# Shift and scale of an expert layer's tokens: from full-width rows to per-feature columns

## The chip, the core and the metric

The kernel runs on one core of a Trainium2 chip. The metric is device microseconds of one execution. The chip works through five engines that run side by side, each through its own queue: TensorE (PE, with its weight loads as PEld), VectorE (DVE), ScalarE (ACT), GpSimd (POOL) and SyncE (SP). Sixteen DMA engines move data between HBM and the on-chip memory SBUF; transfers are issued from the queues of SP, ACT and POOL. TensorE writes to PSUM, which DVE and ACT read.

## The reference

The model is three transformer-like blocks over 256 tokens of 1024 features. Each block has a mixer and, behind it, a mixture of experts; the change lies in how the tokens reach the experts:

```python
h2 = _rms(x) * norm2_w * (1.0 + sc2) + sh2          # shift and scale per feature
x = x + g2 * hier_moe(h2, ...)                      # 32 experts, 2 per token, d_ff 512
...
h = modulate(rms_norm(x, norm_ffn_g[i]), sh2, sc2)  # h * (1 + scale) + shift
x = x + g2[:, None, :] * hier_moe_2(h, ...)         # 16 experts, 2 per token, d_ff 256
```

So a token's input to its experts is `x * r * s + sh`, where `r` is one number per token (the reciprocal root mean square), and `s` and `sh` are one number per feature.

## The kernel before

`body` (line 2314) runs `block1`, an expert phase (`moe_phase`, line 1870, called m1 here after its tile names), the mixer `mla`, a second expert phase (n0), the mixer `hyena`, and a third (n1). The 256 tokens stand as two tiles of 128 partitions, `x[:, t]`, with 1024 features each.

An expert phase works as follows. The weights of its experts stream through a ring of six slots of 2 MB, which SP loads in order as slots come free (`moe_stream`, line 1819): 201 MB in m1, 50 MB in n0 and n1 each. At the start, GpSimd fills a tile `zero`, writes it to the buffer `Y` in HBM (four transfers of 512 KB), and loads two rows of 1024 values from HBM, `shrow` and `srow`, each spread over all 128 partitions (512 KB a row, `row_in`, line 857, called at line 1922). These rows were written to HBM earlier by `moe_prep` (line 864) through `rows_out` (line 845), which transposes 16 columns of 128 on TensorE, copies them on ScalarE and stores them from GpSimd's queue. The same values stand in SBUF as columns: tile `mcols`, one value per feature, eight columns each for the shift and the scale.

`ffn_in` (line 1754) computes `r` (`rms_rows`, a chain of small VectorE instructions, lines 742 to 764), transposes the tokens, scales them by the columns while they leave PSUM, and makes the router's logits on TensorE (line 1773). `ffn_rows` (line 1777) makes the experts' input for all tokens: GpSimd multiplies by `srow` (line 1783), VectorE by `r` and adds `shrow` (line 1784), ScalarE rounds to the matmul's type (`h2h`, line 1786). `Route.choose` (line 137) picks two experts per token, on VectorE and with five small matmuls; `onehot` (line 222) makes the gathering matrix. Behind it the remainder `h2l = h - h2h` is taken, for one token tile on VectorE and for the other on GpSimd (line 1931, by the constant `LOP`).

`Moe.start` (line 495) then gathers the tokens of the first eight experts. For each of eight k-tiles of 128 features, four matmuls (`gather`, line 251: `h2h` and `h2l`, two token tiles) fill a PSUM bank of 128 features by 512 slots, and ScalarE copies it to a tile `xg` (`gathered`, line 263). Only then does the first expert's product with its weights begin (`up_unit`, line 287). Later groups of eight experts are gathered between the experts' matmuls (line 545): three groups in m1, one in n0 and n1 each. The order of each engine's instructions is fixed at build time: the framework places them, `tc.issue_after` puts a block behind a named instruction of the same engine, and the expert loop keeps the written order.

Of the kernel before, what the change touches and what calls it, by code (L numbers as in the profile page):

```python
# [15 lines left out]
F32 = mybir.dt.float32  # L16
# [4 lines left out]
AF = mybir.ActivationFunctionType  # L21
ALU = mybir.AluOpType
# [4 lines left out]
D = 1024  # L27
T = 256
P = 128
# [192 lines left out]
def onehot(k, pool, r, g, tag):  # L222

    oh = k.t(pool, [P, 2, GE, CAP], F32R, tag)
    for t in range(2):
        k.chosen = k.nc.vector.tensor_tensor(
            oh[:, t], r.posm[:, t, g * GE:(g + 1) * GE, None].to_broadcast([P, GE, CAP]),
            k.io64[:, None, :].to_broadcast([P, GE, CAP]), op=ALU.is_equal)
    return oh


class Moe:
# [30 lines left out]
    def gathered(self, g, c, n=None):  # L263

        k, nc = self.k, self.nc
        n = n or GE
        xg = self.xg[g][c] = k.t(self.sb, [P, n * CAP], F32, "xg", bufs=XG)
        self.gathers = nc.scalar.activation(xg, self.gp, AF.Copy)  # L268

    def state(self, e):  # L270
        return self.st.setdefault(e, {})
# [573 lines left out]
def rows_out(k, pool, cols, name):  # L845

    nc, n = k.nc, cols.shape[1]
    d = k.tc.dram_tile([n, P], F32, name=name)
    pt = k.fbank()
    nc.tensor.transpose(pt[:n, :P], cols, k.ident)  # L850
    s = k.t(pool, [n, P], F32, "rowst")
    nc.scalar.copy(s, pt[:n, :P])
    nc.gpsimd.dma_start(d, s)
    return d.rearrange("(n c) p -> n (c p)", c=8)


def row_in(k, pool, d, i, name):

    o = k.t(pool, [P, D], F32, name)
    k.nc.gpsimd.dma_start(o, d[i:i + 1].broadcast_to([P, D]))  # L860
    return o


def moe_prep(k, pool, l, g, ada, wr, br):

    nc, NL = k.nc, wr.shape[2]
    cols = k.t(k.const, [P, 16], F32, f"mcols{l}")
    nc.vector.tensor_copy(cols[:, 0:8], ada[:, 24:32])
    nc.vector.scalar_tensor_tensor(cols[:, 8:16], ada[:, 32:40], 1.0, g, op0=ALU.add, op1=ALU.mult)
    pt = k.fbank()  # L870
    for c in range(8):
        nc.tensor.matmul(pt[:, :NL], ada[:, 24 + c:25 + c].to_broadcast([P, P]), wr[:, c], start=(c == 0), stop=(c == 7))
    crow = k.t(k.const, [P, NL], F32, f"crow{l}")
    nc.vector.tensor_tensor(crow, pt[:, :NL], br, op=ALU.add)
    return dict(s=cols[:, 8:16], crow=crow, rows=rows_out(k, pool, cols, f"mrows{l}"), wr=wr)


def cond_pads(k, cs):
# [449 lines left out]

FTK = 2
EVD = '0123'  # L1330
PSTT = 0
AHEAD = 0

TWO_PI = (6.28125, 0.0019350051879882812, float(2 * np.pi - 6.28125 - 0.0019350051879882812))
# [439 lines left out]
    return pl, r  # L1774


def ffn_rows(k, tmp, x, r, srow, shrow, h2h):

    nc = k.nc
    hs = []  # L1780
    for t in range(2):
        h = k.t(tmp, [P, D], F32, "h2", bufs=2)
        k.rowed = nc.gpsimd.tensor_tensor(h, x[:, t], srow, op=ALU.mult)
        i = (nc.gpsimd if PSTT else nc.vector).scalar_tensor_tensor(h, h, r[:, t:t + 1], shrow, op0=ALU.mult, op1=ALU.add)
        k.rowed = i if PSTT else k.rowed
        nc.scalar.activation(h2h[:, t], h, AF.Copy)  # L1786
        hs.append(h)
    return hs


PLAN = "rrrraaaarafaaarffaaaaafa|ooaooao"
# [9 lines left out]
NRB = 2  # L1801
ORD = "3f2f4ffhckrff1f0f"
FB = [1, 2, 2, 2]
LOP = [1]
MAN = ['None', '0', '1']
RINGS = {'n0': 6, 'n1': 6}

# [62 lines left out]
def moe_phase(k, I, x, l, M, after=None, store=None):  # L1870

    nc, tc = k.nc, k.tc
    NE, FF = (32, 512) if l is None else (16, 256)
    pre = "m1" if l is None else f"n{l}"
    with ExitStack() as es:
        ph = Phase(k, es)
        k.psum(es, acc=4, bank=4)
        k.fill = "acc"
        hp = ph(pre + "h")
        if l is None:  # L1880
            ring = [ph(f"ring{i}") for i in range(4)] + [ph(f"ring{i}", side="right") for i in range(4, 6)]
            S = Stream(k, es, "ring", 6, 4096, homes=[ring[int(c)] for c in RO])
        else:
            S = Stream(k, es, "ring", RINGS[pre], 4096)
        moe_stream(k, I, S, l)
        S.upto(S.depth + len(S.once))
        views = {}

        def load(kind, e, u):

            key = (kind, e, u // 4 if kind == "d" else u // 2) if l is None else (kind, e)
            if key not in views:
                views[key] = S.get(key)
            v = views[key]
            if kind != "d":
                return (lambda a, c: v[:, a, c % 4]) if l is None else (lambda a, c: v[:, c, a * 256:(a + 1) * 256])
            return v[:, :, u % 4] if l is None else v[:, u // 2, :, u % 2]

        def fetch(w, kind, e, u):
            if l is None and kind == "d":  # L1900
                h, c = divmod(u, 2)
                src = I["w2"][ds(e, 1), h][:, :, 2 * c:2 * c + 2]
            elif l is None:
                src = I["w13"][ds(e, 1), u // 2][:, :, "gu".index(kind), u % 2 * 2:u % 2 * 2 + 2]
            elif kind == "d":
                src = I["moe_w_down_2"][l, ds(e, 1), u]
            else:
                src = I["moe_w_in"][l, ds(e, 1)][:, :, 2 * u:2 * u + 2]
            nc.sync.dma_start(w, src.rearrange("a p c f -> p (a c) f"))

        h2h, h2l = k.t(hp, [P, 2, D], F32R, "h2h"), k.t(hp, [P, 2, D], F32R, "h2l")
        with ExitStack() as e1:
            if l is None:
                k.t(ph("pad", es=e1), [P, PAD * 256], F32, "pad")
            rp = ph(pre + "r", es=e1, side="left" if l is None else "right")
            tmp = ph(pre + "t", es=e1)
            Y = tc.dram_tile([2 * T, D], F32, name=pre + "Y")
            zero = k.t(rp, [P, D], F32, "zero")
            nc.gpsimd.memset(zero, 0.0)
            for c in range(2 * T // P):  # L1920
                nc.gpsimd.dma_start(Y[c * P:(c + 1) * P], zero)
            shrow, srow = (row_in(k, rp, M["rows"], i, n) for i, n in enumerate(("shrow", "srow")))
            pl, r = ffn_in(k, tmp, rp if l is None else tmp, x, M)
            R = Route(k, hp, NE, NE // 4, pre)
            hs = ffn_rows(k, tmp, x, r, srow, shrow, h2h)
            R.choose(pl, r, M["crow"])
            oh = onehot(k, hp, R, 0, "oh0")
            with tc.issue_after(k.chosen.ins):
                last = k.rowed
                for t in range(2):  # L1930
                    i = (nc.gpsimd if t in LOP else nc.vector).tensor_tensor(h2l[:, t], hs[t], h2h[:, t].bitcast(F32), op=ALU.subtract)  # L1931
                    if t in LOP:
                        last = i
                    else:
                        low = i
        with ExitStack() as e1:
            m = Moe(k, e1, pre, R, h2h, h2l, load, NE, FF, Y)
            m.fetch = fetch
            m.low = low
            m.start(oh)  # L1940
            with tc.issue_after(m.gathers.ins):
                R.gates()
            run = m.run()
            with (tc.manual_schedule() if str(l) in MAN else ExitStack()):
                next(run)
            if after:
                with tc.issue_after(m.ready.ins), tc.issue_after(last.ins), ExitStack() as e2:
                    after(ph("pl", 2, es=e2))
            with (tc.manual_schedule() if str(l) in MAN else ExitStack()):
                list(run)  # L1950
            op = m.vpool = ph(pre + "o", es=e1)
            with tc.issue_after(last.ins):
                g2 = row_in(k, op, M["g2"], 0, "g2row")
            for h, t in ((0, 0), (0, 1), (1, 0), (1, 1)):
                y, c = k.t(op, [P, 2, 512], F32, "vw", bufs=2), slice(h * 512, (h + 1) * 512)
                with tc.issue_after(m.sent.ins):
                    nc.gpsimd.dma_start(y, Y.rearrange("(c t p) d -> t p c d", c=2, p=P)[t][:, :, c])
                with tc.issue_after(m.acted.ins):
                    nc.vector.tensor_tensor(y[:, 0], y[:, 0], y[:, 1], op=ALU.add)
                    nc.vector.tensor_tensor(y[:, 0], y[:, 0], g2[:, c], op=ALU.mult)  # L1960
                    nc.vector.tensor_tensor(x[:, t, c], x[:, t, c], y[:, 0], op=ALU.add)

            def add():
                for h in range(2):
                    residual(k, op, x, [m.acc[t][h] for t in range(2)], g2, h)
                    if store:
                        store(h)

            add()
            m.overflow(add)  # L1970
            k.newt = None
# [404 lines left out]
```

## Time and profile before

| What | Value |
|---|---|
| median of three runs | 1531.34 us (1524.98 to 1534.3) |
| the profiled execution | 1536.42 us, of which the span in the profile is 1534.7 us |
| busy share of the span: PE, DVE, ACT, POOL | 86%, 36%, 30%, 8% |
| TensorE's mean granted clock | 0.922 of full speed |
| moved by DMA | 462.18 MB, 301 GB/s over the span |
| experts begin (first line 287): m1, n0, n1 | 346.74, 1078.37, 1409.62 us |

Times inside the profile count from the start of the span. The share of busy time is a mean over stages with different limits, so each expert phase is read by itself. In the rows below, a name such as `h<-xres,srow` gives the tile written and the tiles read, and a bracket at the end of a timeline row says how long the engine had been idle and what ended that.

### The profile page before, as it was taken

To read this page: it belongs to the slowest core of one execution; us is meant where nothing else is said; L and a number is where in the kernel's file an instruction comes from. 1 tells how busy PE (TensorE), PEld (TensorE's weight loads), DVE (VectorE), ACT (ScalarE), POOL (GpSimd) and SP (SyncE) were. 2 spreads that over 40 slices of the span, in tenths; PEclk is the share of its full clock that TensorE was granted. 3 is DMA by queue.
4 is the path that set the end of the run, shared out by engine and by line. 5 is a ranking of instruction groups with operands and counts; after the bars stand their busy time and mean duration, and the time that the engine had idled before them with its cause. 6 is when DMAs were issued, how large, how long until landed. Compare 5 with 4: busy or idle time off the path is not lost. (4 is left out here: it accounts for less than half of the span.)

```text
span 1534.7 us, 18651 instructions
## 1 busy us (share of the span) xinstructions
PE 1319.7 (86%) x7228; PEld 761.0 (50%) x7228; DVE 546.5 (36%) x1522; ACT 461.6 (30%) x906; POOL 116.2 (8%) x153
## 2 busy tenths in 40 slices
PE   5898999939989999989988397991999399987995
PEld 2676686623345453323322164661554388766552
DVE  2563665440321320000000556442102577765004
ACT  2463343311223322112111253430232255423221
POOL 0000000020111210000000100011001000102000
PEclk9799899959999999999999688995999599997998
DMA  8457714458998999999999567476799665729996
GB/s 330 174 201 258 265 66 165 172 217 351 414 400 337 345 336 421 424 425 424 425 424 423 216 236 258 165 262 272 309 418 417 230 245 204 263 104 384 410 420 235
DMA packets 65904, 462.18 MB, mean 301 GB/s; under 512 B 9782, under 2 KB 10134, under 8 KB 33680
## 3 DMA queue, kind: packets, MB, share of 16 engines
q1 hardware_dynamic: 52496, 424.97, 70.2%
q0 software_dynamic: 12880, 35.21, 6.1%
q8 instruction: 60, 0.98, 0.3%
q10 hardware_dynamic: 432, 0.72, 0.2%
q14 instruction: 36, 0.29, 0.1%
HBM read 444.04 MB, written 25.74 MB: 306 GB/s over the span
## 5 line engine op out<-in xcount | busy, mean ns | idle before, releaser
L287 PE MATMUL bank<-ring,xg 128*64 128x512 f32 (+1 forms) x2048 | 354.3, 491 | 19.1 <-DMA ring<-in_w_dram 16.6
L287 PEld LDWEIGHTS bank<-ring,xg 128*64 128x64 f32 x2048 | 142.2, 137 | 205.7 <-issue 135.4
L377 PE MATMUL bank<-ring,a 128*64 128x512 f32 x768 | 204.9, 602 | 7.6 <-DMA ring<-in_w_dram 7.5
L310 DVE TENSOR_TENSOR a<-bank,sg 128x256 f32<-128x256 f32 (+1 forms) x64 | 22.9, 358 | 475.0 <-ACT sg L305 290.3
L818 DVE TENSOR_TENSOR wl<-ra,wh 128x1024 fp32r<-128x1024 f32 (+1 forms) x77 | 93.3, 1216 | 77.7 <-ACT wh L816 76.7
L816 ACT ACTIVATE wh<-ra 128x1024 fp32r<-128x1024 f32 (+1 forms) x77 | 80.7, 1053 | 112.6 <-PE acc L831 38.5
L377 PEld LDWEIGHTS bank<-ring,a 128*64 128x64 f32 x768 | 55.1, 136 | 103.2 <-issue 88.0
L292 ACT ACTIVATE s<-bank 128x512 f32<-128x512 f32 (+1 forms) x64 | 31.4, 491 | 248.7 <-PE bank L287 248.7
L898 PE MATMUL fill<-rb,cpad 128*32 128x512 f32 x384 | 67.8, 655 | 27.4 <-DMA rb<-in_ada_w_dram 19.6
L259 PE MATMUL bank<-oh,h2h 128*128 128x512 f32 x128 | 48.1, 459 | 48.4 <-ACT h2h L1786 47.3
L366 ACT ACTIVATE y<-bank,gts 128x512 f32<-128x512 f32 x54 | 37.1, 688 | 75.9 <-PE bank L377 75.9
L268 ACT ACTIVATE xg<-bank 128x512 f32<-128x512 f32 x64 | 38.3, 598 | 68.8 <-PE bank L259 68.8
L259 PEld LDWEIGHTS bank<-oh,h2h 128*128 128x128 f32 x128 | 25.0, 213 | 66.9 <-ACT h2h L1786 48.9
L1688 PE MATMUL acc<-hTh,wh 128*128 128x256 f32 x192 | 55.7, 293 | 0.0
L1688 PE MATMUL acc<-hTh,wl 128*128 128x256 f32 x192 | 55.4, 294 | 0.2 <-DVE wl L818 0.2
L1688 PE MATMUL acc<-hTl,wh 128*128 128x256 f32 x192 | 54.1, 285 | 0.0
L305 ACT ACTIVATE sg<-bank 128x256 f32<-128x256 f32 (+1 forms) x64 | 21.0, 328 | 91.6 <-PE bank L299 91.6
L259 PE MATMUL bank<-oh,h2l 128*128 128x512 f32 x128 | 44.3, 432 | 1.6 <-POOL h2l L1931 1.6
L299 PEld LDWEIGHTS bank<-ident,s 128*128 128x128 f32 x192 | 19.8, 140 | 46.3 <-issue 36.2
L831 PE MATMUL acc<-wh,hTh 128*128 128x512 f32 (+1 forms) x96 | 39.6, 412 | 3.6 <-ACT hTv L800 3.6
L1662 PE MATMUL acc<-ftk,dftf 128*128 128x128 f32 x256 | 36.0, 287 | 7.6 <-ACT ftk L1656 7.6
L1662 PEld LDWEIGHTS acc<-ftk,dftf 128*128 128x128 f32 x256 | 30.8, 192 | 22.1 <-ACT ftk L1656 12.0
(689 smaller groups left out, 2132.3 us busy)
## 6 DMA issues: line engine op xcount, KB each, us to landing
ring<-in_w_dram SPq DMA_DIRECT2D x64, 2048.0 KB, 18.9
ring<-in_moe_w_in_dram SPq DMA_DIRECT2D x32, 2048.0 KB, 17.6
ring<-in_w_dram SPq DMA_DIRECT2D x62, 1024.0 KB, 17.8
rb<-in_ada_w_dram SPq DMA_DIRECT2D x48, 1024.0 KB, 5.2
ring<-in_moe_w_down_dram SPq DMA_DIRECT2D x32, 1024.0 KB, 18.6
rb<-in_w_mod_dram SPq DMA_DIRECT2D x16, 1024.0 KB, 7.6
ra<-in_hy_w_in_dram SPq DMA_DIRECT2D x12, 1024.0 KB, 8.8
ra<-in_w_in_dram SPq DMA_DIRECT2D x20, 512.0 KB, 3.8
```

The source lines that it names most:

```text
L259: i = nc.tensor.matmul(self.gp, h[:, t, c * P:(c + 1) * P], oh[:, t], start=(a == t == 0), stop=(a == t == 1))
L268: self.gathers = nc.scalar.activation(xg, self.gp, AF.Copy)
L287: self.nc.tensor.matmul(s["p"][a * CAP:(a + 1) * CAP, :self.FF], x, w(a, c), start=(c == 0), stop=(c == 7))
L292: self.nc.scalar.activation(s["s"], s["p"][:, :self.FF], AF.Copy)
L366: nc.scalar.activation(s["y"][:, h * 512:(h + 1) * 512], s["d", h], AF.Copy, scale=s["gt"])
L377: self.nc.tensor.matmul(q["d", h][i * CAP:(i + 1) * CAP], self.state(2 * p + i)["av"][:, c], w[:, i], start=(c == 0), stop=(c == nk - 1))
L816: k.last[0] = k.nc.scalar.activation(wh[:, :, :n], w, AF.Copy)
L818: k.last[1] = k.nc.vector.tensor_tensor(wl[:, :, :n], w, wh[:, :, :n].bitcast(F32), op=ALU.subtract)
L831: k.last[2] = k.nc.tensor.matmul(out, x, y[:, j, c0:c0 + n], start=(kt == 0 and a == 0), stop=(kt == KT - 1 and a == 2))
L898: nc.tensor.matmul(pr[32 * g:32 * g + 32], k.cpad[:, l, 4 * q + g], wq[:, g], start=(q == 0), stop=(q == 1))
L1662: nc.tensor.matmul(pt[:, (2 * f + n) * P:(2 * f + n + 1) * P], self.fwd[:, t, n, f * P:(f + 1) * P], tk[:, n, t], start=(t == 0), stop=(t ...
L1688: nc.tensor.matmul(acc[i][:, :T], y[:, jj, i * P:(i + 1) * P], self.hT[x][:, kt], start=(kt == 0 and a == 0), stop=(kt == 7 and a == 2))
```

## The change

The rows are dropped. The tokens are only normalised before the gather (`x * r`, on ScalarE, straight into `h2h`), and their remainder is taken on VectorE by one instruction per half tile, `x * r - h2h`, behind the gathering matrix. The scale and the shift are applied as the gathered k-tile leaves PSUM: there the features lie on partitions, so ScalarE takes both as one value per partition. A gathered slot that no token fills now holds the shift instead of zero; its output goes nowhere, as before. `rows_out` of the 16 columns, both `row_in` loads, GpSimd's products and its half of the remainder go away.

```diff
     def gathered(self, g, c, n=None):
-        self.gathers = nc.scalar.activation(xg, self.gp, AF.Copy)
+        self.gathers = nc.scalar.activation(xg, self.gp, AF.Identity, scale=self.scale[:, c:c + 1], bias=self.shift[:, c:c + 1])
...
     # moe_prep
-    return dict(s=cols[:, 8:16], crow=crow, rows=rows_out(k, pool, cols, f"mrows{l}"), wr=wr)
+    return dict(s=cols[:, 8:16], sh=cols[:, 0:8], crow=crow, wr=wr)
...
-def ffn_rows(k, tmp, x, r, srow, shrow, h2h):
+def ffn_rows(k, x, r, h2h, h2l):
     nc = k.nc
-    hs = []
     for t in range(2):
-        h = k.t(tmp, [P, D], F32, "h2", bufs=2)
-        k.rowed = nc.gpsimd.tensor_tensor(h, x[:, t], srow, op=ALU.mult)
-        i = (nc.gpsimd if PSTT else nc.vector).scalar_tensor_tensor(h, h, r[:, t:t + 1], shrow, op0=ALU.mult, op1=ALU.add)
-        k.rowed = i if PSTT else k.rowed
-        nc.scalar.activation(h2h[:, t], h, AF.Copy)
-        hs.append(h)
-    return hs
+        nc.scalar.activation(h2h[:, t], x[:, t], AF.Copy, scale=r[:, t:t + 1])
+
+    def second():
+        for h in range(2):
+            for t in range(2):
+                c = slice(h * 512, (h + 1) * 512)
+                i = nc.vector.scalar_tensor_tensor(h2l[:, t, c], x[:, t, c], r[:, t:t + 1], h2h[:, t, c].bitcast(F32),
+                                                   op0=ALU.mult, op1=ALU.subtract)
+        return i
+    return second
...
     # moe_phase
-            shrow, srow = (row_in(k, rp, M["rows"], i, n) for i, n in enumerate(("shrow", "srow")))
             pl, r = ffn_in(k, tmp, rp if l is None else tmp, x, M)
             R = Route(k, hp, NE, NE // 4, pre)
-            hs = ffn_rows(k, tmp, x, r, srow, shrow, h2h)
+            second = ffn_rows(k, x, r, h2h, h2l)
             R.choose(pl, r, M["crow"])
             oh = onehot(k, hp, R, 0, "oh0")
             with tc.issue_after(k.chosen.ins):
-                last = k.rowed
-                for t in range(2):
-                    i = (nc.gpsimd if t in LOP else nc.vector).tensor_tensor(h2l[:, t], hs[t], h2h[:, t].bitcast(F32), op=ALU.subtract)
-                    if t in LOP:
-                        last = i
-                    else:
-                        low = i
+                last = second()
...
             m.fetch = fetch
-            m.low = low
+            m.scale, m.shift = M["s"], M["sh"]
```

## Rows read from the trace of the kernel before

**Rows 1.** Waits in n0: engine, tile, line <- releaser: us, times, longest.
```profile
POOL h L1783 <- DMA srow<-mrows: 26.3, 1, 26.3
```

**Rows 2.** Timeline of m1's start: start us, us, engine, line, operation [idle before <-releaser].
```profile
315.03 1.29 DVE L226 TENSOR_TENSOR oh<-m1posm,io 128x512 fp32r<-128x512 f32 x2
...
327.30 4.64 POOL L1783 TENSOR_TENSOR h<-xres,srow 128x1024 f32<-128x1024 f32 x2 [19.80 <-DMA srow<-mrows]
...
333.05 2.25 ACT L1786 ACTIVATE h2h<-h 128x1024 fp32r<-128x1024 f32 x2 [24.26 <-DVE h L1784]
...
334.16 1.99 PE L259 MATMUL bank<-oh,h2h 128*128 128x512 f32 x3 [19.43 <-ACT h2h L1786]
...
346.74 10.52 PE L287 MATMUL bank<-ring,xg 128*64 128x512 f32 x48
```

**Rows 3.** Windows in m1: length, busy us PE PEld DVE ACT POOL, clock, DMA, GB/s.
```profile
323.00:326.00 3.00, 0.00 (x0) 0.00 (x0) 0.00 (x0) 0.00 (x0) 0.00 (x0) 0.50 0.92 377
...
328.00:336.00 8.00, 1.84 (x4) 1.05 (x5) 6.29 (x4) 2.11 (x2) 4.56 (x3) 0.50 0.00 0
```

**Rows 4.** Timeline of n0's start, same columns as rows 2.
```profile
1032.07 0.16 DVE L749 TENSOR_SCALAR rxi<-rxv 128x2 int32<-128x2 int32 x1
...
1039.16 1.29 DVE L226 TENSOR_TENSOR oh<-n0posm,io 128x512 fp32r<-128x512 f32 x2
...
1066.77 1.99 PE L259 MATMUL bank<-oh,h2h 128*128 128x512 f32 x3 [27.87 <-ACT h2h L1786]
...
1078.37 5.40 PE L287 MATMUL bank<-ring,xg 128*64 128x256 f32 x48
...
1082.08 1.54 SPq L1841 DMA_DIRECT2D ring<-in_moe_w_down_dram  x2
```

**Rows 5.** Windows of n0's wait and gather, same columns as rows 3.
```profile
1058.00:1060.00 2.00, 0.00 (x0) 0.00 (x0) 0.00 (x0) 0.00 (x0) 0.10 (x1) 0.50 0.96 410
...
1061.00:1070.00 9.00, 2.84 (x5) 1.33 (x5) 5.70 (x3) 2.12 (x2) 5.55 (x3) 0.50 0.01 5
...
1073.00:1074.00 1.00, 1.00 (x4) 0.76 (x4) 0.00 (x0) 0.18 (x1) 0.00 (x0) 0.67 0.21 86
```

**Rows 6.** Timeline of n1's start and one row of its end, same columns as rows 2.
```profile
1382.90 5.05 POOL L1783 TENSOR_TENSOR h<-xres,srow 128x1024 f32<-128x1024 f32 x2 [0.45 <-DVE xres L842]
...
1384.28 1.38 DVE L742 SCALAR_TENSOR_TENSOR rxv<-rxq 128x2 f32<-128x2 f32 x1
...
1385.97 2.01 DVE L749 TENSOR_SCALAR rxi<-rxv 128x2 int32<-128x2 int32 x1
...
1390.29 2.48 DVE L1784 SCALAR_TENSOR_TENSOR h<-h,rxy,shrow 128x1024 f32<-128x1024 f32 x2
...
1394.32 2.01 DVE L124 TENSOR_TENSOR n1ae<-n1ae,n1af 128x40 f32<-128x40 f32 x1
...
1398.83 1.29 DVE L226 TENSOR_TENSOR oh<-n1posm,io 128x512 fp32r<-128x512 f32 x2
...
1399.67 2.04 PE L259 MATMUL bank<-oh,h2h 128*128 128x512 f32 x4 [1.10 <-DVE oh L226]
...
1409.62 5.40 PE L287 MATMUL bank<-ring,xg 128*64 128x256 f32 x48
...
1508.00 1.95 PE L287 MATMUL bank<-ring,xg 128*64 128x256 f32 x16 [0.52 <-DMA ring<-in_moe_w_in_dram]
```

**Rows 7.** A window of n1, same columns as rows 3.
```profile
1410.00:1415.00 5.00, 5.00 (x49) 3.12 (x45) 1.48 (x9) 3.49 (x6) 0.00 (x0) 1.00 0.52 212
```

**Rows 8.** ScalarE's groups: line, operation, shapes, count | busy us, mean ns | idle.
```profile
L268 ACT ACTIVATE xg<-bank 128x512 f32<-128x512 f32 x64 | 38.3, 598 | 68.8 <-PE bank L259 68.8
...
L292 ACT ACTIVATE s<-bank 128x256 f32<-128x256 f32 x32 | 12.3, 385 | 77.5 <-PE bank L287 77.5
...
L305 ACT ACT_TABLE_LOAD x3 | 3.8, 1283 | 0.1
...
L800 ACT ACTIVATE hTv<-bank,ada,s 128x256 f32<-128x256 f32 x16 | 8.6, 562 | 12.3 <-PE bank L796 9.2 <-DVE hTl L802 3.0
```

More of the change, by code (lines that the diff above doesn't have):

```diff
@@ L1330 @@
 EVD = '0123'
-PSTT = 0
 AHEAD = 0
@@ L1803 @@
 FB = [1, 2, 2, 2]
-LOP = [1]
 MAN = ['None', '0', '1']
```

## The prediction

> **What bounds the kernel now.** TensorE is busy 86% of the span and the DMA engines nearly as long, so the share table does not say where time can be won. I went to the start of each expert phase instead and read the waits, then the timeline engine by engine, then the windows.
>
> The waits say that GpSimd's product on line 1783 stood 26.3 us for the transfer of `srow` in n0 [rows 1], and the timeline of m1 shows the same with 19.80 us [rows 2]. What hangs on it: in m1 the gathering matrix is written from 315.03 to 316.32, but the first gather starts at 334.16, after the row (327.30), two products, two passes of line 1784 and the first rounding (333.05 on), and its last operand, GpSimd's half of `h2l`, comes later still; the first expert starts at 346.74 [rows 2]. n0 repeats it: matrix at 1039.16, gather at 1066.77, expert at 1078.37 [rows 4]. In n1 the row was loaded long before, and the gather follows its matrix after 0.84 us (1398.83 to 1399.67) [rows 6]. So two of three phases start late by a transfer that is queued among the ring's first loads.
>
> Does the late start cost anything where DMA is the limit? The windows answer. The backlog ends about 326 in m1; from 328 to 336 DMA moves nothing [rows 3]. In n0 it ends about 1060, and from 1061 to 1070 DMA is busy 0.01 [rows 5]. The ring is full, and its next load goes out only when the first expert has used a slot, 3.71 us after its start (1078.37 to 1082.08) [rows 4]. TensorE and DMA wait together, so a start that comes earlier moves both.
>
> **The change, part by part.** The sum is made against the profiled execution, 1536.4 us (span 1534.7), which is 5.1 us above the median of the runs, 1531.3.
>
> *The start of m1.* `h2h` now needs only `r`, which the router's chain needs too, so its two passes (2.25 us together, rows 2) end inside that chain. The gather then waits for the matrix alone: 315.03 + 0.84 (n1's distance) = 315.87. `second` puts four half-tile instructions behind the matrix; line 1784 takes 2.48 for two full tiles [rows 6], so 0.62 each. The first two are done at 316.32 + 1.24 = 317.6, about when TensorE has done the first four matmuls on `h2h` (n1 takes 2.04 for them); the rest follows far ahead of k-tile 4. Gather to first expert took 9.95 us in n1 (1399.67 to 1409.62) [rows 6]. In m1 and n0 TensorE starts it from a standstill at the half clock (1.2 GHz): n0's gather began at 1066.77 and the grant rose only inside the window at 1073 [rows 5]. n0's own took 11.6 with a wait for GpSimd's half of `h2l` in it. I take 10.6, between the two. With 0.17 for the last eviction (below) the experts start at 315.87 + 10.6 + 0.17 = 326.6, 20.1 us earlier. DMA: the backlog loses two rows of 0.5 MB, 2.5 us at 410 GB/s [rows 5], so it ends near 323.5, before the slot freed at 330.3. Both limits move by 20.1. I take 20.
>
> *The start of n0.* 1039.16 + 0.84 + 10.6 + 0.17 = 1050.8, against 1078.37: 27.6 us for TensorE. Here the backlog is longer: it ends at 1060 - 2.5 = 1057.5, behind the first freed slot (1054.5), so DMA runs on without a gap. Before, it took up work again about 1 us behind 1082.08, say 1083. DMA therefore gains 25.5, less 1.2 if the 0.5 MB of `g2row`, now free to be issued sooner, joins the backlog: 24.3. If TensorE remains the limit, 27.6; if DMA becomes it, 24.3. I take 26.
>
> *The start of n1.* Nothing waits for a row here, but GpSimd's work held up VectorE. While line 1783 ran (1382.90 to 1387.95), two instructions on two columns took 1.38 and 2.01 and ended as the GpSimd instructions did; line 124 took 2.01 beside GpSimd's `h2l` [rows 6]. With GpSimd idle line 749 took 0.16 [rows 4]. The three stand in the chain to the matrix: 1.2 + 1.85 + 1.8 = 4.9 us. Line 1784, on VectorE between `r` and the logits, goes too, but the logits came no earlier. TensorE gains 4.9. DMA gains less: the transfers paused for only 2.4 us (5 us at a share of 0.52) [rows 7], and near the end an expert waits for its weights (0.52) [rows 6]. So 2.4 by DMA, 4.9 by TensorE; I take 2.5, by the limit that is waited for.
>
> The Trainium skill ("GPSIMD Engine Reference", section 1, Specifications) says that GpSimd shares its SBUF interfaces with VectorE and that VectorE instructions with two SBUF inputs contend. The trace agrees (line 124, with two, took 2.01 us) and goes further: line 749, with one, was held as long. Against the change the rule says that `second`, which reads `x` and `h2h`, would be held by any GpSimd work beside it: one such hold in each phase would make the sum 6 us less, none leaves it, since GpSimd then has only transfers to issue there.
>
> *The eviction.* 64 instructions on line 268 get two per-partition values. Copy without them takes 598 ns; at 256 columns the plain form takes 385 and one with both 562 [rows 8], so +0.177 each, 0.775 in all. In the starting gather a k-tile takes TensorE four matmuls (on average 1.2 us in n1, 9.95 for eight), so ScalarE keeps up and only the last one shows. In the 40 later ones TensorE sometimes waits on `xg`: 0 to 7 us, and since m1's 24 lie where weights are awaited, I take 1 lost.
>
> *The rest.* `rows_out` goes three times, one short transpose, one copy and one transfer each among other work: between 0 and 0.5 us, taken as 0. The later `g2row` and filter loads move forward on GpSimd's queue, past nothing that waits: 0.
>
> Sum: 20 + 26 + 2.5 - 1 = 47.5. 1536.4 - 47.5 = 1488.9; on the median, 1531.3 - 47.5 = **1484**. Bounds: with gathers of 9.95 us and TensorE as the limit throughout, 20.7 + 28.3 + 4.9 + 0.5 = 54.4 gained (1477); with gathers of 11.6, DMA as the limit in n0, nothing in n1 and every later eviction on the path, 19.1 + 24.3 + 0 - 7 = 36.4 (1495).
>
> **Rivals.**
> *The wait is replaced.* The gather's tiles take memory that the `zero` tile or its transfers still hold, or the ring's first loads arrive late, so the gather starts as the backlog ends: 323.5 and 1057.5. Experts then start at 334.3 and 1068.3, gaining 12.4 and 10; with n1 and the eviction 24, so 1507. For it: all these transfers share one backlog. Against: in m1 the memory below is padded, and no row shows such a wait. 8%.
> *`h2l` is late.* VectorE places the counting instructions or others ahead of `second`, or it is held; 2 to 3 us in each phase: 40 gained, 1491. 7%.
> *Slower: table loads.* If Identity needed another function table than Silu, each of the 40 later evictions could force a change there and back, at 1.283 us each [rows 8]: 103 us of ScalarE between an expert's product and its Silu. It decides from the point where TensorE waits for 47.5 of the 103 us; with all of them waited for, the time is 1484 + 103 = 1587. Against: the loads on line 305 are three, one a phase, and no load group stands at line 800, an Identity. 3%. The Trainium skill ("ScalarE: Activation LUTs", section "Table sets: the hidden batching unit") has identity in every set, which would rule this out, and a load near 2.7 us; the trace agrees on the first as far as line 800 goes, and its 1.283 us stands for the second.
> *It does not do what it says.* Something beside the row holds the start just as long: 1529. Against: each link of the chain in rows 2 names the next. 2%.
>
> **Numbers.** My forecast, 1477 to 1495, has 80%; the rivals 8, 7, 3 and 2. The measurement of this kernel tells about 1% (15 us) from no change. Faster by over 1%: 80 + 8 + 7 = 95%; within 1%: 2%; slower: 3%. The range has to hold 8 in 10 and the runs before spread by 9 us, so I widen it to 1474 to 1500.
>
> **What would show it.** Right: the first line 259 within 2 us of the gathering matrix in all three phases; first experts 20, 46 and 49 us earlier; no idle DMA in n0's start and some 5 us in m1's; line 742, 749 and 124 near 0.2 us in n1; line 268 at 0.77 us with no table load beside it. Wrong: gathers that wait for a transfer or for `second`, ring loads that experts now wait for in n0, or a phase whose end has not moved with its start.

## The result and the profile after

The changed kernel takes 1474.95 us (median of 4, 1470.14 to 1478.32) against 1529.44 for the kernel before in the same comparison (1524.98 to 1534.3): a ratio of 0.963, 95% interval 0.9606 to 0.9653. A second comparison below gave 1477.66 against 1531.15, ratio 0.9649 (0.9627 to 0.9671). So 54.5 us are gained where 47.5 were forecast. The time lies 9 us under the forecast of 1484, 2 us under the 1477 to 1495 that were given 80%, and 1 us inside the widened 1474 to 1500; the second comparison's lies inside both. The direction and the mechanism were forecast, and the size was too small.

The profiled execution took 1470.14 us, span 1468.4. It is the quickest of the four, and the one profiled before (1536.42) was slower than any of those timed, so this pair of traces differs by 66 us, 12 more than the medians do. The table below shows where most of those 12 lie.

The timeline of m1's start, after (line 259 is the gather, 288 the first expert's product, 1787 the remainder), answers to [rows 2]:

```profile
312.55 1.29 DVE L226 TENSOR_TENSOR oh<-m1posm,io 128x512 fp32r<-128x512 f32 x2
313.39 1.62 PE L259 MATMUL bank<-oh,h2h 128*128 128x512 f32 x3 [1.13 <-DVE oh L226]
313.76 2.74 DVE L1787 SCALAR_TENSOR_TENSOR h2l<-xres,rxy,h2h 128x512 fp32r<-128x512 f32 x4
...
322.83 4.51 PE L288 MATMUL bank<-ring,xg 128*64 128x512 f32 x20
...
326.52 0.80 SPq L1853 DMA_DIRECT2D ring<-in_w_dram  x2
```

The bracket of the gather now names the matrix, 0.84 us after its start, and the remainder (0.75 us for each half tile, where 0.62 was forecast) holds TensorE up once in each start, for 0.3 us. Matrix to first expert is 10.28 us; it was 31.71. The same stretch of n0, for [rows 4]:

```profile
1008.85 1.29 DVE L226 TENSOR_TENSOR oh<-n0posm,io 128x512 fp32r<-128x512 f32 x2
1009.69 1.62 PE L259 MATMUL bank<-oh,h2h 128*128 128x512 f32 x3 [1.10 <-DVE oh L226]
...
1019.16 5.18 PE L288 MATMUL bank<-ring,xg 128*64 128x256 f32 x46
1022.87 0.89 SPq L1842 DMA_DIRECT2D ring<-in_moe_w_down_dram  x2
```

Matrix to first expert: 10.31 us, was 39.21; and as before the ring's next load follows 3.71 us behind it. And n1, for [rows 6]:

```profile
1321.62 0.16 DVE L743 SCALAR_TENSOR_TENSOR rxv<-rxq 128x2 f32<-128x2 f32 x1
1322.33 0.16 DVE L750 TENSOR_SCALAR rxi<-rxv 128x2 int32<-128x2 int32 x1
...
1329.22 0.24 DVE L143 SCALAR_TENSOR_TENSOR n1lg<-bank,rxy,crow 128x20 f32<-128x20 f32 x1 [4.02 <-PE bank L1773]
...
1330.85 0.20 DVE L124 TENSOR_TENSOR n1ae<-n1ae,n1af 128x40 f32<-128x40 f32 x1
...
1333.57 1.29 DVE L226 TENSOR_TENSOR oh<-n1posm,io 128x512 fp32r<-128x512 f32 x2
...
1343.67 2.60 PE L288 MATMUL bank<-ring,xg 128*64 128x256 f32 x22
```

The three held instructions are back at 0.16, 0.16 and 0.20 us. But see the bracket on line 143, where VectorE takes up the router's logits: it waits 4.02 us for TensorE. That wait matters below.

Windows of the two starts (length, busy us of PE, PEld, DVE, ACT, POOL, granted clock, DMA share, GB/s), for [rows 3] and [rows 5]:

```profile
313.00:318.00 5.00, 4.61 (x12) 3.59 (x13) 4.14 (x11) 1.56 (x2) 0.61 (x1) 0.56 0.98 358
318.00:321.00 3.00, 3.00 (x15) 2.43 (x14) 0.00 (x0) 2.34 (x3) 0.00 (x0) 1.00 1.00 408
321.00:326.00 5.00, 5.00 (x25) 2.37 (x25) 1.65 (x9) 2.52 (x5) 0.00 (x0) 1.00 0.39 151
326.00:328.00 2.00, 2.00 (x12) 0.60 (x10) 0.00 (x0) 0.00 (x0) 0.00 (x0) 1.00 0.34 49
...
1010.00:1015.00 5.00, 5.00 (x15) 3.81 (x15) 3.32 (x9) 1.90 (x3) 0.00 (x0) 0.63 1.03 421
1015.00:1020.00 5.00, 5.00 (x27) 3.67 (x27) 0.00 (x0) 4.29 (x7) 0.00 (x0) 1.00 1.05 436
```

DMA is idle for about 4.4 us in m1's start (0.61 of 5 and 0.66 of 2) and not at all in n0's. The clock column is read thus: a mean of 0.56 over 5 us between the levels 0.5 and 1.0 puts the return to full clock 0.6 us before the window's end, at 317.4, 4.0 us behind the first gather; n0's 0.63 gives 1013.7, again 4.0 us behind it.

The eviction and the table loads, by ScalarE's groups (times, busy us, mean ns):

```profile
L269 ACT ACTIVATE xg<-bank,mcols 128x512 f32<-128x512 f32 x64 | 49.8, 778 | 66.6 <-PE bank L259 63.7
...
L306 ACT ACT_TABLE_LOAD x3 | 3.8, 1283 | 0.1
```

TensorE also waits longer than before in front of the experts' products in the last third of n0 (us, times, longest):

```profile
PE bank L288 <- SPq L413: 1.6, 1, 1.6
PE bank L288 <- DMA ring<-in_moe_w_in_dram: 1.6, 2, 1.2
```

Half of these 3.2 us are put down to ring loads, the other half to SyncE's queue (line 413). The kernel before has one such wait there, of 0.6 us.

### The profile page after: what moved, and what is told of

It is laid out like the page before. It is cut to its first block, busy times and chain, and to the rows that moved or that the text cites. A ratio compares the mean times of both kernels' runs of the same rounds, so it can differ in the third digit from the quotient of the medians.

```text
span 1468.4 us, 18609 instructions
## 1 busy us (share of the span) xinstructions
PE 1307.5 (89%) x7225; PEld 754.8 (51%) x7225; DVE 532.4 (36%) x1525; ACT 471.8 (32%) x903; POOL 90.0 (6%) x135
## 5 line engine op out<-in xcount | busy, mean ns | idle before, releaser
L269 ACT ACTIVATE xg<-bank,mcols 128x512 f32<-128x512 f32 x64 | 49.8, 778 | 66.6 <-PE bank L259 63.7
L1662 PEld LDWEIGHTS acc<-ftk,dftf 128*128 128x128 f32 x256 | 30.8, 192 | 22.2 <-ACT ftk L1656 12.1
L832 PE MATMUL acc<-wh,hTl 128*128 128x512 f32 (+1 forms) x96 | 38.5, 401 | 0.0
```

Of the source, the lines that this page charges most:

```text
L269: self.gathers = nc.scalar.activation(xg, self.gp, AF.Identity, scale=self.scale[:, c:c + 1], bias=self.shift[:, c:c + 1])
L832: k.last[2] = k.nc.tensor.matmul(out, x, y[:, j, c0:c0 + n], start=(kt == 0 and a == 0), stop=(kt == KT - 1 and a == 2))
L1662: nc.tensor.matmul(pt[:, (2 * f + n) * P:(2 * f + n + 1) * P], self.fwd[:, t, n, f * P:(f + 1) * P], tk[:, n, t], start=(t == 0), stop=(t ...
```

## The experiments

Each trace was cut at the same marks of its timeline: a "start" runs from the first transposition of the router (line 1766) to the first expert's product, the "rest" of a phase from there to the first matmul of the next mixer (line 797, 796 in the kernels of before, or the end), and "mixers" is what is left (`block1`, `mla`, `hyena`). In the changed kernel's first trace the marks are 301.63, 322.83, 855.7, 997.48, 1019.16, 1154.53, 1318.52, 1343.67 and the end. In us:

| trace | m1 start | n0 start | n1 start | m1 rest | n0 rest | n1 rest | mixers | span |
|---|---|---|---|---|---|---|---|---|
| before | 42.6 | 49.9 | 28.4 | 535.6 | 135.2 | 125.0 | 617.8 | 1534.7 |
| before, again | 43.0 | 50.9 | 28.7 | 534.0 | 135.2 | 126.9 | 610.6 | 1529.3 |
| before, both halves on VectorE | 40.5 | 52.2 | 25.9 | 536.1 | 135.3 | 125.0 | 612.1 | 1527.0 |
| before, constant rows | 27.8 | 30.9 | 28.8 | 532.6 | 137.1 | 124.3 | 607.6 | 1489.1 |
| changed | 21.2 | 21.7 | 25.2 | 532.9 | 135.4 | 124.7 | 607.4 | 1468.4 |
| changed, again | 21.2 | 21.7 | 25.3 | 535.2 | 135.3 | 125.0 | 611.4 | 1475.1 |
| rows stored | 21.2 | 21.7 | 25.1 | 535.0 | 135.8 | 124.6 | 608.6 | 1472.0 |
| rows stored and loaded | 21.2 | 21.7 | 25.2 | 533.0 | 140.7 | 124.8 | 609.5 | 1476.2 |
| plain copy | 21.2 | 21.6 | 25.1 | 534.9 | 136.3 | 124.4 | 611.0 | 1474.5 |
| GpSimd products | 27.2 | 25.3 | 25.9 | 534.8 | 136.7 | 125.6 | 610.8 | 1486.2 |
| one GpSimd product | 23.9 | 24.4 | 23.7 | 533.5 | 137.2 | 126.7 | 605.8 | 1475.2 |
| VectorE passes | 23.6 | 22.2 | 25.1 | 537.1 | 135.0 | 124.6 | 610.0 | 1477.6 |
| early zeros | 21.2 | 21.6 | 25.3 | 533.0 | 135.6 | 124.6 | 622.7 | 1484.1 |

### Both kernels again

> The changed kernel once more, unchanged, to see which differences of the first pair of traces repeat. Theory A (the mixers really became shorter, because the stores of the rows, their transposes and copies left them): 1475 within 3 us, and in the trace the stretches outside the three starts are shorter than before by about as much as in the first trace (2 to 4 us each in block1, mla and hyena). Theory B (only the three starts changed, and the rest of the first pair's 66 us was one fast profile set against a slow one): the same median, but a trace in which block1, mla and hyena take within 1 us what they took before. Theory C (each start simply gained 1 to 2 us more than I summed and the evictions cost nothing): the same median, starts that gain 21 to 22, 27 to 28 and 3 to 4 us, in all runs alike.

> The kernel before once more, unchanged, for a second trace. All theories: a median of 1529 within 4 us. A: block1, mla and hyena take within 1 us what they took in its first trace. B: they differ from the first trace by 2 us or more, and so do the stretches at the half clock. C: says nothing of the mixers; first experts at 31.7 us behind the gathering matrix in m1 and 39 in n0, as before.

Measured: 1477.66 us (1474.12 to 1478.86), and 1533.47 (1525.66 to 1538.82; 0.5 above the stretch expected) beside 1531.15 for the reference runs of before. The starts repeat to 0.1 us in the changed kernel and to 1 us in the old one. The mixers do not repeat: 617.8 and 610.6 before, 607.4 and 611.4 changed. Most of the first pair's surplus is that one 617.8; this is Theory B. Why the mixers differ from one execution to the next stays open. Over all traces whose mixers hold the old code, 607.6 to 617.8; with the new code (without the early zeros), 605.8 to 611.4. A difference of some 3 us between the means stays possible and is not shown. The starts speak for Theory C: their gains, by the means of the two traces each, are 21.6, 28.7 and 3.4 us, together 53.7; the medians of this comparison differ by 53.5.

### The stores of the rows, put back

```diff
-    return dict(s=cols[:, 8:16], sh=cols[:, 0:8], crow=crow, wr=wr)
+    return dict(s=cols[:, 8:16], sh=cols[:, 0:8], crow=crow, rows=rows_out(k, pool, cols, f"mrows{l}"), wr=wr)
```

> The changed kernel with the three stores of the modulation rows put back (transpose, copy, transfer); nobody reads them. A: 3 to 8 us slower than the changed kernel, lost in block1, mla and hyena. B and C, and my prediction's term (0 to 0.5 us): within 1 us of it.

Measured: 1476.72 us, ratio 0.9645 (0.9618 to 0.9673), beside 0.9649 for the changed kernel. So no run shows the 3 to 8 us of Theory A, and the term taken as 0 stands, as closely as the comparison can tell (some 4 us).

### The eviction as a plain copy

```diff
-        self.gathers = nc.scalar.activation(xg, self.gp, AF.Identity, scale=self.scale[:, c:c + 1], bias=self.shift[:, c:c + 1])
+        self.gathers = nc.scalar.activation(xg, self.gp, AF.Copy)
```

> The changed kernel with the eviction as a plain copy; scale and shift of the experts' input are left out. The eviction returns to 0.60 us. My prediction's term: 1 us faster in all, 0.17 in each start and the rest in m1's 24 later evictions. C: no difference within 0.5 us beyond the 0.17 of each start. If the second bound of that term were right, 7 us faster.

Measured: 1476.31 us, ratio 0.9645 (0.9622 to 0.9667). ScalarE's group of evictions:

```profile
L269 ACT ACTIVATE xg<-bank 128x512 f32<-128x512 f32 x64 | 38.3, 598 | 74.8 <-PE bank L259 74.6
```

The two values per partition cost 180 ns each time, 11.5 us of ScalarE's time in all, and next to nothing of the kernel's: at most 0.2 us in a start, and m1's rest (534.9) lies between those of the two changed traces (532.9 and 535.2). The 1.35 us between the medians is less than the comparison can tell.

### Rows without transfers

The kernel before, with its rows from constants:

```diff
-            shrow, srow = (row_in(k, rp, M["rows"], i, n) for i, n in enumerate(("shrow", "srow")))
+            shrow, srow = (k.t(rp, [P, D], F32, n) for n in ("shrow", "srow"))
+            nc.gpsimd.memset(shrow, 0.0)
+            nc.gpsimd.memset(srow, 1.0)
```

> The kernel before, with the two rows filled on chip (ones and zeros) in place of their loads, so the values of scale and shift are left out; products, remainder halves and order stay. Theory W (the transfer was the wait, and what is left of the old chain costs in m1 and n0 what it costs in n1, where the changed kernel gained 3.4 us): router to first expert 24.6 us in m1 (42.8 before, 21.2 changed), 25.1 in n0 (50.4, 21.7), 28.6 in n1 as before; about 43 us faster than the kernel before, 1488. Rival V (the rest of the chain, GpSimd's products and its half of the remainder, cost more than the transfer): starts of 30 us or more in m1 and n0, 1500 or above.

Measured: 1493.6 us, ratio 0.9765 (0.974 to 0.9791): 37.2 us faster than before. The timeline of its m1 start (line 1786 rounds, 1933 is the remainder, 287 the first expert):

```profile
304.79 4.65 POOL L1783 TENSOR_TENSOR h<-xres,srow 128x1024 f32<-128x1024 f32 x2
...
316.24 2.47 DVE L1784 SCALAR_TENSOR_TENSOR h<-h,rxy,shrow 128x1024 f32<-128x1024 f32 x2
317.55 2.25 ACT L1786 ACTIVATE h2h<-h 128x1024 fp32r<-128x1024 f32 x2 [12.12 <-DVE h L1784]
...
319.88 2.80 POOL L1933 TENSOR_TENSOR h2l<-h,h2h 128x1024 fp32r<-128x1024 f32 x1 [10.44 <-ACT h2h L1786]
...
328.52 1.94 PE L287 MATMUL bank<-ring,xg 128*64 128x512 f32 x8
```

The transfer was the larger part: 15.0 us of m1's 21.6 and 19.5 of n0's 28.7 go with it alone. Theory W was too small for the rest (6.6 and 9.2 us, where I expected 3.4): with the product early, line 1784 ran behind the choice of experts in m1 (316.24), and the rounding behind that again. n0's start (30.9) even reaches Rival V's 30, but what is left of the chain costs less than the transfer in both phases, and the kernel stays under Rival V's 1500.

### What held n1

Four kernels take apart the 3.4 us of n1. First, the kernel before with both halves of the remainder on VectorE:

```diff
-LOP = [1]
+LOP = []
...
-                last = k.rowed
...
                     else:
-                        low = i
+                        low = last = i
```

> The kernel before with both halves of the remainder on VectorE (GpSimd's half taken away), rows and their transfers as before. If GpSimd's half held line 124 in n1's chain: 124 goes from 2.0 to 0.2 us and the matrix stands 1.8 us sooner behind the router; in m1 and n0 the transfer stays the wait and they start as before. Total 1527 to 1530. If the hold were not in the chain: n1 as before.

Measured: 1530.18 us, ratio 0.9996 (0.9978 to 1.0014). n1's timeline:

```profile
1385.22 2.48 DVE L1784 SCALAR_TENSOR_TENSOR h<-h,rxy,shrow 128x1024 f32<-128x1024 f32 x2
1387.64 0.24 DVE L143 SCALAR_TENSOR_TENSOR n1lg<-bank,rxy,crow 128x20 f32<-128x20 f32 x1
...
1389.27 0.20 DVE L124 TENSOR_TENSOR n1ae<-n1ae,n1af 128x40 f32<-128x40 f32 x1
...
1391.97 1.29 DVE L226 TENSOR_TENSOR oh<-n1posm,io 128x512 fp32r<-128x512 f32 x2
```

Line 124 takes 0.20 and n1's start drops by 2.7 us, most of what the whole change brings there: the gather begins 1.8 us sooner behind the router, as expected, and takes 0.8 to 1.1 us less. Yet the kernel is no faster by a measurable amount: m1's start gains 2.3, but n0's loses 1.8. Its wait for the row grew:

```profile
POOL h L1783 <- DMA srow<-mrows: 30.0, 1, 30.0
```

It was 26.3 [rows 1]. Without GpSimd's half, the load of `g2row` is issued ahead of the row on the same queue (at 1021.81, `srow` at 1025.94), and the wait is 3.7 us longer; in the second trace of before it was 26.0. `g2row`'s 0.5 MB alone are 1.3 us at 410 GB/s, so the rest of the 3.7 is not explained.

Second, the changed kernel with the two products back on GpSimd:

```diff
+            for t in range(2):
+                d = k.t(tmp, [P, D], F32, "h2", bufs=2)
+                nc.gpsimd.tensor_tensor(d, x[:, t], x[:, t], op=ALU.mult)
             second = ffn_rows(k, x, r, h2h, h2l)
```

> The changed kernel with two GpSimd products over the tokens put beside the router, result unused. If GpSimd's work holds VectorE's chain in every start: lines 743 and 750 go from 0.16 to 1.4 to 2 us, the starts get 3 to 5 us longer in all three phases, 1485 to 1490. If it held only in n1 by an accident of order: one start alone, about 1479.

Measured: 1488.94 us, ratio 0.9736 (0.9711 to 0.9761). The starts are longer by 6.0, 3.6 and 0.7 us. VectorE in m1 and in n1:

```profile
306.45 2.68 DVE L743 SCALAR_TENSOR_TENSOR rxv<-rxq 128x2 f32<-128x2 f32 x1
...
1337.86 0.91 DVE L743 SCALAR_TENSOR_TENSOR rxv<-rxq 128x2 f32<-128x2 f32 x1
...
1339.09 1.55 DVE L750 TENSOR_SCALAR rxi<-rxv 128x2 int32<-128x2 int32 x1
...
1345.36 0.24 DVE L143 SCALAR_TENSOR_TENSOR n1lg<-bank,rxy,crow 128x20 f32<-128x20 f32 x1 [2.51 <-PE bank L1773]
```

Both theories were half right: VectorE is held in every phase (in n0 lines 743 and 750 take 1.56 and 1.86 us), but in n1 it still has 2.51 us to wait for the logits behind the holds, so there they cost almost nothing. By themselves, then, the holds of lines 742 and 749 in n1 [rows 6] were not in the chain; that of line 124, behind the logits, was. Together with line 1784 they were in it by a little: in the kernel before, and in the one with both halves on VectorE, line 143 follows line 1784 without waiting for TensorE, 11.5 us behind the router's first transposition, and in the changed kernel it comes 10.3 to 10.7 us behind it.

Third and fourth, one GpSimd product beside the choice, and two VectorE passes ahead of the logits:

```diff
+            d = k.t(tmp, [P, D], F32, "h2")
+            nc.gpsimd.tensor_tensor(d, x[:, 1], h2h[:, 1].bitcast(F32), op=ALU.subtract)
             R.choose(pl, r, M["crow"])
```

> The changed kernel with one GpSimd product over a token tile behind the rounded tokens, beside the choice of experts, result unused. If a GpSimd instruction with two inputs stops VectorE wherever they meet: one VectorE instruction of 1.5 to 2 us in each choice, each start 1.5 to 2 us longer, 1481. If it is absorbed as the two products were in n1: 1476.

```diff
+            for t in range(2):
+                d = k.t(tmp, [P, D], F32, "h2", bufs=2)
+                nc.vector.scalar_tensor_tensor(d, x[:, t], r[:, t:t + 1], x[:, t], op0=ALU.mult, op1=ALU.add)
             R.choose(pl, r, M["crow"])
```

> The changed kernel with two full VectorE passes (about 2.5 us) between r and the logits, result unused, where line 1784 stood in the kernel before. If the logits leave TensorE later than r in every phase: less than 1 us each, 1477. If VectorE is the chain there: 2.5 us each, 1484. From n1's rows (11.5 us from router to first logits line before, 10.7 changed) I expect 0.8 us in n1 and 1.5 to 2.5 in m1 and n0, where logits come at the full clock.

Measured: 1478.48 us (ratio 0.9654, 0.9613 to 0.9695) and 1479.31 (0.9654, 0.9615 to 0.9692). Neither total can be told from the changed kernel's; the starts can. The single product lengthens those of m1 and n0 by 2.7 us each. n1's is 1.5 us shorter: TensorE's mean granted clock over it was 0.71 (0.66 in both traces of the changed kernel), and the logits came 9.6 us behind the router's first transposition. Why the clock differed there is open. Line 124 in its m1, by the timeline:

```profile
307.00 2.36 DVE L124 TENSOR_TENSOR m1ae<-m1ae,m1af 128x80 f32<-128x80 f32 x1
```

In its n1 most of the product (line 1927) fell into VectorE's wait for the logits, and line 143, which reads the logits from PSUM, was not held in the middle of it:

```profile
1333.04 2.34 POOL L1927 TENSOR_TENSOR h<-xres,h2h 128x1024 f32<-128x1024 f32 x1 [0.34 <-ACT h2h L1781]
1334.40 0.24 DVE L143 SCALAR_TENSOR_TENSOR n1lg<-bank,rxy,crow 128x20 f32<-128x20 f32 x1 [3.67 <-PE bank L1773]
1334.83 0.24 DVE L143 SCALAR_TENSOR_TENSOR n1lg<-bank,rxy,crow 128x20 f32<-128x20 f32 x1 [0.19 <-PE bank L1773]
...
1336.03 0.20 DVE L124 TENSOR_TENSOR n1ae<-n1ae,n1af 128x40 f32<-128x40 f32 x1
```

The passes cost 2.4 us in m1, 0.5 in n0 and nothing in n1, where I had expected 1.5 to 2.5 in the first two and 0.8 in n1, whose waits still show line 143 waiting for TensorE:

```profile
DVE n1lg L143 <- PE bank L1773: 1.7, 2, 1.5
```

### DMA in n0's start

The rows stored and loaded again, read by nobody (on top of the stores put back):

```diff
+            shrow, srow = (row_in(k, rp, M["rows"], i, n) for i, n in enumerate(("shrow", "srow")))
             pl, r = ffn_in(k, tmp, rp if l is None else tmp, x, M)
```

> The changed kernel with the rows stored and loaded again, 1 MB more in each start's backlog, and read by nobody. If DMA has room in the starts: no more than 1 us. If DMA is the limit in n0 (its last expert waits for weights in the changed kernel, 2.6 us given back there): n0's end 2.5 us later, most of it made good before the next mixer starts, m1 and n1 unchanged; 1476 to 1479.

Measured: 1480.41 us, ratio 0.9674 (0.965 to 0.9698), 2.8 above the changed kernel by the medians of two comparisons, whose intervals overlap. The starts are untouched, so it was the wait for the row and not its bytes that held them. In the one trace n0's rest is 5.3 us longer, outside the 135.0 to 137.2 of all others, and nothing of it is made good. TensorE's waits in n0, and a window behind them:

```profile
PE bank L288 <- DMA ring<-in_moe_w_in_dram: 4.1, 3, 1.6
PE bank L288 <- SPq L413: 2.1, 1, 2.1
```

```profile
1124.00:1128.00 4.00, 3.63 (x17) 1.80 (x17) 0.00 (x0) 0.00 (x0) 0.00 (x0) 0.57 1.03 403
```

The bytes alone are 2.5 us at 410 GB/s, as I had it. In this trace the waits were followed by a stretch at a mean grant of 0.57 (in the changed kernel's second trace the same stretch, 1122 to 1126, was at 1.00), so matmuls at half the clock come on top. TensorE's waits are 6.2 us here and 3.2 in the changed kernel.

### A try at a faster kernel

```diff
     # moe_prep, in place of the tile and the four writes in moe_phase
+    if not hasattr(k, "zero"):
+        k.zero = k.t(k.const, [P, P], F32, "zero")
+        nc.gpsimd.memset(k.zero, 0.0)
+    Y = k.tc.dram_tile([2 * T, D], F32, name=f"Y{l}")
+    for c in range(2 * T // P):
+        nc.gpsimd.dma_start(Y[c * P:(c + 1) * P].rearrange("p (a d) -> p a d", d=P), k.zero[:, None, :].to_broadcast([P, 8, P]))
...
+            Y = M["Y"]
```

> A try at a faster kernel: the zeros of the buffer Y (2 MB a phase) are written in the mixers, from a constant tile, in place of the start's backlog. If the backlog still limits n0's end: its 2.6 us come back, m1 and n1 stay; 1473 to 1475. If the writes cost the mixers' loads their place: 0 to 5 us slower than the changed kernel. If TensorE alone is the limit: the same.

Measured: 1487.88 us, ratio 0.9731 (0.9705 to 0.9758), 10 us slower than the changed kernel. The listing of `Y` (ns, then first and last start):

```profile
L881 POOL DMA_DIRECT2D Y<-zero x12: 847/858/1287, 4.2 to 25.8; - x12
```

Nothing held the writes back, so all twelve went out in the first 26 us, among the first weights of `block1`, whose end came 12 us later (the mixers' 622.7). Apart from that accident: n0's experts ended 2.6 us sooner behind its first expert than in the changed kernel (107.5 us to 110.1), but the combining behind them took as much longer, so n0's rest (135.6) did not move, nor did n1's. Those bytes do not set the end of these phases, and a version that holds the writes back was not tried.

What the combining waits for in n0 is the transfer that reads `Y` back, before and after:

```profile
1198.11 0.69 DVE L1959 TENSOR_TENSOR vw<-vw 128x512 f32<-128x512 f32 x1 [6.16 <-DMA vw<-n0Y]
...
1138.76 0.69 DVE L1953 TENSOR_TENSOR vw<-vw 128x512 f32<-128x512 f32 x1 [4.84 <-DMA vw<-n0Y]
```

VectorE takes up what it brings 119.7 us behind the first expert in the kernel before and 119.6 in the changed one, though the last expert comes 3 us later there: GpSimd issues the transfer 1.2 us later (111.4 us, was 110.2), and it takes as much less. Why it does is open. With the early zeros VectorE goes on at 121.1, and with the rows loaded at 126.2.

## Where the prediction was right, and the step that failed

**Direction and mechanism hold.** The wait for the row was the bound of two starts, and removing it moved both limits. The gather follows its matrix by 0.84 us in all three phases, as taken from n1. `h2h` ends inside the router's chain (in n0 it is written from 1003.31, the matrix from 1008.85), and `second` keeps ahead of TensorE but for 0.3 us. Constant rows show the transfer as the larger part.

**The step that failed is the size of the terms: 20 + 26 + 2.5 - 1 came out as 21.6 + 28.7 + 3.4 + 0, which is 53.7.** The largest error is n0's 26, which took a limit of DMA into the sum that did not bind. That the total comes near the upper bound, 54.4, is in part luck: m1 and n0 gained more than the bound's 20.7 and 28.3, n1 less than its 4.9.

- *The gather, 10.6 us and 0.17.* It took 9.44 in m1 (313.39 to 322.83) and 9.47 in n0 (9.47 and 10.12 in the second trace). I set it between n1's 9.95 and n0's 11.6, since TensorE would start from a standstill at the half clock. It does, but the clock was back 4.0 us behind the first gather (4.1 in m1 and 5.5 in n0 in the second trace); before, in n0, 7 us behind it [rows 4, 5], and in the second trace of before 9.6 us (gather from 1060.5, a mean of 0.81 from 1069 to 1072, so back at 1070.1). The old gathers also waited for GpSimd's half. This is 1.3 us in m1 and in n0 of the first trace.
- *n0, "I take 26".* I averaged 27.6 (TensorE) with 24.3 (DMA). The measured gain is TensorE's. DMA was near: the changed kernel waits 3.2 us in front of its last products, and the experts' stretch is 3 us longer (110.1 us, was 107.0). But the combining behind it, which hangs on the transfer that reads `Y` back, is as much shorter (25.3, was 28.2), so the rest of n0 is 135.2 us before and 135.4 after, and the start's gain is kept whole. I had no term for what comes behind the last expert. With 1 MB more, in one trace, VectorE gets `Y` 6.6 us later and 5.3 us are lost and kept.
- *n1, 2.5.* Right for neither of its reasons. TensorE's 4.9 counted three holds as one chain. Two of them lie ahead of the logits, and my reading that line 1784 did not make the logits' use later was wrong: these three together made line 143 some 1.0 us later (11.5 us behind the router's first transposition, 10.7 and 10.3 in the changed kernel), and neither the holds alone nor the passes alone do. The hold behind the logits, of line 124, is worth 1.8, and the gather is 0.6 us shorter by the means of two traces each: together 3.4. DMA's 2.4, which cut it, did not bind: the rest of n1 is no longer than before.
- *The eviction, -1.* 0.778 us against the forecast 0.775, but hidden: the plain copy gains no measurable time. The 1 was my choice out of 0 to 7, without a row that gave it.
- *`rows_out`, 0.* Nothing measurable, as forecast.

**The rivals.** No gather waited for the backlog, `second` was not late, and there is no table load beside line 269: the group on line 306 still counts three. The Trainium skill ("ScalarE: Activation LUTs", section "Table sets: the hidden batching unit") has identity in every set; the trace agrees, with 64 evictions and no load of their own.

The hold of VectorE was right as a mechanism, and so was its price in m1 and n0: I had put 2 us on one hold in each phase, and one GpSimd product put back costs 2.7, 2.7 and, in n1, nothing. The Trainium skill ("GPSIMD Engine Reference", section 1, Specifications) names two kinds of VectorE instructions that contend: those with two SBUF inputs and those in a 2-port perf mode. The trace agrees for the first kind: line 743, which adds two halves of `rxq`, took 2.68 us beside GpSimd's product and 0.16 without it. Line 750 has one input and took 1.55 beside it; I called that more than the rule says, and left out the rule's second kind. Whether lines 749 and 750 ran in such a mode no row here shows.

**The list of signs.** Gathers at the matrix, 4.4 us of idle DMA in m1 and none in n0, line 743, 750 and 124 at 0.16 to 0.20, the eviction at 0.778: all as forecast. First experts were to be 20, 46 and 49 us earlier; in the first pair of traces they are 23.9, 59.2 and 65.9 earlier, which holds the mixers of that one trace, too. By the starts alone it is 21.6, 50.3 and 53.7.

## What to carry to other kernels

When a value per feature is applied to token rows, ask whether the tile passes PSUM with the features on partitions anyway: there scale and shift ride on an eviction (0.18 us for both, hidden here), and a broadcast load that queues behind the weights is gone. When a start moves, price the phase from its start to the next phase's first work, and ask what its end waits for: here it was a transfer behind the experts that came no later, so what the experts lost to DMA cost nothing, and averaging that limit into the sum made the forecast too small. Take two traces of each kernel, cut at the same marks, before a difference outside the change is explained.

## What the hardware showed that was not expected

- A GpSimd product can hold one small VectorE instruction for 0.9 to 2.7 us (lines 124, 743 and 750), though not each: line 143 took its 0.24 us in the middle of one. The price depends on what is late: 6.0 us in m1, 3.6 in n0, 0.7 in n1 for the same two products.
- With a load issued ahead of it on GpSimd's queue, a transfer came later than the added bytes account for: with `g2row` ahead of `srow`, n0's wait was 30.0 us instead of 26.3 and 26.0 (one trace against two).
- With 1 MB of loads that nobody reads, 2.5 us at 410 GB/s, n0 was 5.3 us longer in the one trace, with a granted clock of 0.57 behind TensorE's waits.
- The mixers, with the same code, took 617.8 and 610.6 us in two traces of one kernel (607.6 to 617.8 over the four kernels that hold it), with starts that repeat to 1 us.
